# Hybrid decoder block, MLP stages: operands refilled two tiles to a slot, weight sums kept in DRAM, down's first units held in up's buffers

## The chip, the cores and the metric

The kernel runs on one core of one Trainium2 chip. The time is the device time of one execution in microseconds (us); the time of a kernel is the median of its runs. Everything is computed in float32.

## The reference

One layer of a decoder trunk over S = 2048 tokens of width D = 1024. The first half (projection, dilated attention, pooling groups) is not touched. What the change touches is the MLP behind it, with D_FF = 2816:

```python
h = h + concatenate([att, pool]) @ w_out
hn = _rmsnorm(h, ln_ffn)
up = _causal_dwconv(hn @ w_up, conv_w, conv_b)     # width 3, along the tokens, 2 * D_FF channels
gate, val = split(up, 2)
h = h + (silu(gate) * val) @ w_down
g = sigmoid(_rmsnorm(h, ln_ple) @ w_ple_gate)
h = h + g * (p @ w_ple)
return _rmsnorm(h, ln_final)
```

## The kernel before, in words

**Exact products.** Every float32 operand is split into a high part (a cast to fp32r by ScalarE, L83) and a low part (operand minus high part, a subtraction by VectorE or GpSimd, L84). A product is then three matmuls: high by high, high by low, low by high (L88 to L90 in `mm3`, L1236 in `product`). So each tile that TensorE uses needs one cast and one subtraction first.

**Stages.** Projection and attention come first. `phase_rest` then holds out projection, up, down, gate and final norm, one after the other.

**Out projection.** Four chunks of 512 tokens (`c`), each in two groups of four output banks (`grp`), eight steps of the contraction in the order 4, 5, 6, 7, 0, 1, 2, 3. The weights lie in a ring of ten tiles with the tag `w` (five pairs of high and low part) and a few more. A group's end adds the residual on VectorE, stores the new h (`h1`) through ScalarE's queue (L1118) and squares it on ScalarE (L153) for the norm; four steps later one-column matmuls (`st`, L99) sum the squares.

**Up's operands.** Up is computed by a Strassen-like scheme: the tokens fall into two halves of 1024, each half and the 1024 features of hn into 2 by 2 blocks, and seven products of block sums take the place of eight. `prepare(half)` normalises h1 and forms the seven operands a11, a12, a22, s1, s2, s3, s4, each of four tiles of 128 x 512. For half 0 it runs during the last chunks of the out projection: a11, s2, s1 and s4 are split at once and stay on the chip; a12, s3 and a22 go to DRAM (`g.op`). For half 1 all seven go to DRAM. `prepare` is a list of 22 small steps (`todo`), and two more are put in as it runs; in up, `product` pops one of them for each product from turn 1 on.

**Up.** 44 turns: two halves by 22 blocks of 128 gate channels and 128 value channels. A turn has seven slots, one product of 12 matmuls each, with these operands and weight blocks:

```text
slot 0  a11 x b11      slot 1  a22 x t4 (of the turn before)   slot 2  s2 x t2
slot 3  a12 x b21      slot 4  s1 x t1       slot 5  s3 x t3     slot 6  s4 x b22
```

Two weight tiles of 512 KB are loaded for a turn (`raw_load`, two turns ahead). GpSimd forms the sums t1, t3 (tile t13), t2 (in place in the first raw tile) and t4 (L1205 to L1207, L1214), again in half 1 as in half 0. The blocks are split in three pairs and one single (`split_w`). Slots 0, 2, 4 and 6 gather in one bank (`ua`), slot 3 in `ub`, slots 5 and 1 in `uc`. Along the way ScalarE copies the bank out before the next product is added (ug after slot 0, L1334, and after slot 2, L1352; uv after slot 4 and slot 6), so slot 2 cannot start before the ug copy; VectorE adds the other banks (L1261); the width-3 convolution is one scaled copy on ScalarE (`conv_a`, L1247) and four or two instructions on VectorE (`conv_b`, L1251 to L1258); silu, the product yg x yv (L1386), and the store to DRAM (`act`, L1387) follow in the next turn.

**What sets the order in up.** Up stands in a `manual_schedule` of TensorE, ScalarE, VectorE and GpSimd: these four run their instructions in the order in which the code writes them. Only SyncE, which issues most DMAs, is placed by the scheduler. `take_operand` fetches an operand's four tiles from DRAM through a ring of six tiles (`nt`) and splits them in one go, four casts one behind the other (L996) with their subtractions on VectorE and GpSimd in turn (L997). It does so for a12, s3 and a22 in turn 0, and for all seven operands of half 1 in turn 21 (the last, a22, in turn 22).

**Down.** Four chunks of 512 tokens by 22 units of the contraction. A unit is one weight tile (`ahead`, L1417) and one act tile (`act_ahead`, L1426), both loaded three units ahead and split; its seven products go to seven `dn` banks, the eighth to the bank `odd`, three units later (`wait = 3`), since the statistics matmuls of the chunk before (`fin`, two units into the next chunk) use that bank first. In chunk 2 `renorm` begins the norm for the gate; gate and final norm follow.

## Time and profile before

| | |
|---|---|
| runs | 2636.32, 2625.2, 2632.01 us; median 2632.01 |
| profiled execution | 2628.29 us, span in the trace 2626.5 us |
| mean granted clock of TensorE | 0.968 of full speed |
| TensorE busy | 2432.7 us (93% of the span) |
| VectorE, ScalarE, GpSimd busy | 1656.6, 1098.8, 705.3 us |
| out projection's last matmuls | until about 926 us of the span |
| up | about 926 to 1844 us |
| down, then gate and final norm | about 1861 us to the end |

How to read it: the execution's own time is 1.8 us longer than the span that the trace covers, and 3.7 us below the median of the runs. A matmul of 128 x 128 by 128 x 512 at the full clock comes every 0.2267 us. "Idle before" an instruction is the time in which its engine had nothing to do, with the engine or DMA that ended it behind the arrow. The granted clock of a stretch is a share of the full one.

### The profile page before, as it was taken

The page shows a single profiled execution, that of the slowest core. Times are in us where ns is not written, and L with a number is a line of the kernel's source. Part 1 is how long each engine was busy: PE and PEld are TensorE (multiplying, and loading weights), DVE is VectorE, ACT ScalarE, POOL GpSimd, SP SyncE. Part 2 cuts the span into 40 slices and gives each one's busy share as a digit, 9 for nine tenths or more (in the row PEclk, how much of TensorE's full clock was granted, in tenths as well). Part 3 has the DMA queues.
Part 4 walks back from the last instruction along what each step waited for, and adds up shares of the span by engine and source line. Part 5 has one row for each costly group of instructions (what it writes and reads, how often), then busy time and mean ns, then how long its engine had stood idle before and what let it go on. Part 6 is the DMA issues. An engine that isn't in the chain of part 4 may idle for free.

```text
span 2626.5 us, 31943 instructions
## 1 busy us (share of the span) xinstructions
PE 2432.7 (93%) x11515; PEld 2030.2 (77%) x11515; DVE 1656.6 (63%) x2404; ACT 1098.8 (42%) x1923; POOL 705.3 (27%) x534
## 2 busy tenths in 40 slices
PE   8999998877889978999996999999799999998998
PEld 7888887766768867788885877778687878787788
DVE  6635437876852668888887777777334363434655
ACT  5423228876821243444454444444223242323332
POOL 3312220244500152334345333332121222122000
PEclk9999999988989989999997999999899999999999
DMA  7534369768466646322223222221445464535332
GB/s 235 175 125 170 132 206 241 171 178 200 139 227 200 232 136 204 125 96 72 96 89 120 76 93 73 73 96 65 153 145 197 146 213 145 186 129 171 120 107 85
DMA packets 203822, 383.73 MB, mean 146 GB/s; under 512 B 37792, under 2 KB 80416, under 8 KB 200592
## 3 DMA queue, kind: packets, MB, share of 16 engines
q1 hardware_dynamic: 168608, 328.56, 39.8%
q0 software_dynamic: 18912, 25.75, 3.0%
q10 hardware_dynamic: 16144, 27.38, 2.8%
q8 instruction: 91, 1.49, 0.2%
q14 instruction: 67, 0.55, 0.1%
HBM read 272.71 MB, written 108.82 MB: 145 GB/s over the span
## 4 chain that ended last, share of the span: by engine, by line
PE 54%; DVE 14%; issue 11%; ACT 8%; DMA 7%; POOL 2%; SPq 0%; ACTq 0%; POOLq 0%; DVEq 0%
PE ua L1236 9%; PE dn L89 5%; PE dn L88 5%; PE dn L90 5%; PE uc L1236 4%; PE z L90 3%; PE z L88 3%; PE z L89 3%; ACT wu L83 3%; PE ub L1236 2%; DMA wb<-wd 2%; PE o L90 2%; DVE yg L1251 2%; DVE yg L1252 2%; PE o L88 2%
## 5 line engine op out<-in xcount | busy, mean ns | idle before, releaser
L88 PE MATMUL dn<-ah,hd 128*128 128x512 f32 x704 | 277.5, 394 | 16.9 <-ACT ah L83 16.9
L89 PE MATMUL dn<-al,hd 128*128 128x512 f32 x704 | 276.8, 393 | 0.9 <-DVE al L84 0.9
L90 PE MATMUL dn<-ah,ld 128*128 128x512 f32 x704 | 276.5, 393 | 0.0
L84 POOL TENSOR_TENSOR ld<-rd,hd 128x1024 fp32r<-128x1024 f32 x44 | 105.9, 2407 | 437.8 <-ACT hd L83 425.4
L83 ACT CAST hd<-rd 128x1024 fp32r<-128x1024 f32 x88 | 92.6, 1052 | 311.6 <-PE dn L89 171.3
L84 DVE TENSOR_TENSOR al<-ra,ah 128x512 fp32r<-128x512 f32 x88 | 124.5, 1418 | 137.4 <-ACT ah L83 137.4
L88 PE MATMUL z<-hnh,wh 128*128 128x512 f32 (+1 forms) x480 | 171.2, 357 | 9.6 <-ACT hnh L251 6.1
L89 PE MATMUL z<-hnl,wh 128*128 128x512 f32 (+1 forms) x480 | 170.8, 356 | 2.5 <-DVE hnl L252 2.3
L90 PE MATMUL z<-hnh,wl 128*128 128x512 f32 (+1 forms) x480 | 170.6, 355 | 1.7 <-POOL wl L84 1.7
L88 PEld LDWEIGHTS dn<-ah,hd 128*128 128x128 f32 x704 | 134.0, 190 | 45.3 <-ACT ah L83 17.3
L89 PEld LDWEIGHTS dn<-al,hd 128*128 128x128 f32 x704 | 133.9, 190 | 30.0 <-DVE al L84 2.2
L90 PEld LDWEIGHTS dn<-ah,ld 128*128 128x128 f32 x704 | 133.7, 190 | 28.1
L1205 POOL TENSOR_TENSOR t<-ru 128x512 f32<-128x512 f32 x44 | 59.5, 1352 | 350.8 <-DVE wu L84 335.2
L1236 PE MATMUL ua<-s2h,wu 128*128 128x512 f32 x352 | 121.9, 408 | 34.3 <-ACT ug L1334 34.3
L84 DVE TENSOR_TENSOR wu<-ru,wu 128x1024 fp32r<-128x1024 f32 x88 | 119.8, 1362 | 52.8 <-ACT wu L83 52.8
L84 DVE TENSOR_TENSOR wu<-t,wu 128x1024 fp32r<-128x1024 f32 x88 | 87.2, 991 | 100.8 <-ACT wu L83 58.6
L84 DVE TENSOR_TENSOR ld<-rd,hd 128x1024 fp32r<-128x1024 f32 x44 | 53.9, 1224 | 126.2 <-ACT hd L83 125.3
L154 DVE TENSOR_TENSOR acc<-acc,sq 128x512 f32<-128x512 f32 (+1 forms) x125 | 89.8, 719 | 58.3 <-ACT sq L153 46.0
L1236 PE MATMUL uc<-a22h,wu 128*128 128x512 f32 x352 | 118.1, 397 | 8.7 <-DVE uv L1261 8.6
L1236 PE MATMUL ua<-a11h,wu 128*128 128x512 f32 x352 | 117.6, 395 | 9.0 <-ACT wu L83 8.8
L1236 PE MATMUL ua<-s4h,wu 128*128 128x512 f32 x352 | 117.4, 395 | 4.8 <-ACT uv L1375 4.8
L1236 PE MATMUL ub<-a12h,wu 128*128 128x512 f32 x352 | 115.8, 390 | 0.0
(304 smaller groups left out, 6817.7 us busy)
## 6 DMA issues: line engine op xcount, KB each, us to landing
ru<-in_w_up_dram SPq DMA_DIRECT2D x88, 512.0 KB, 3.7
rd<-in_w_down_dram SPq DMA_DIRECT2D x88, 512.0 KB, 3.6
act<-yg SPq DMA_DIRECT2D x44, 512.0 KB, 2.9
ra<-act SPq DMA_DIRECT2D x88, 256.0 KB, 3.7
wr<-in_w_in_dram SPq DMA_DIRECT2D x64, 256.0 KB, 4.0
nt<-h SPq DMA_DIRECT2D x56, 256.0 KB, 3.6
h<-h SPq DMA_DIRECT2D x56, 256.0 KB, 5.2
qhh<-qh SPq DMA_DIRECT2D x16, 512.0 KB, 9.4
```

Of the source, the lines that this page charges most:

```text
L83: nc.scalar.copy(hi, src)
L84: (low or nc.gpsimd).tensor_tensor(lo, src, fp(hi), op=ALU.subtract)
L88: nc.tensor.matmul(ps, wh, ah, start=first, stop=False)
L89: nc.tensor.matmul(ps, wh, al, start=False, stop=False)
L90: nc.tensor.matmul(ps, wl, ah, start=False, stop=last)
L154: nc.vector.tensor_tensor(acc[:, :n], acc[:, :n], sq[:, :n], op=ALU.add)
L1205: eng.tensor_tensor(t13[:, :CH], r0[:, CH:], r0[:, :CH], op=ALU.subtract)
L1236: nc.tensor.matmul(pst, x[:, ksl], y, start=first and k == 0 and n == 0, stop=k == HK - 1 and n == 2, skip_group_check=True)
L1251: nc.vector.scalar_tensor_tensor(y[:, 1:], u[:, : n - 1], coef(f, 1), y[:, 1:], op0=ALU.mult, op1=ALU.add)
L1252: nc.vector.scalar_tensor_tensor(y[:, 2:], u[:, : n - 2], coef(f, 0), y[:, 2:], op0=ALU.mult, op1=ALU.add)
```

## The change

It has six parts. All six are in one kernel.

1. **Turn 0's weights earlier.** `raw_load(0)`, the sums and the splits of turn 0 stand inside the last chunk of the out projection: the sums behind the first group, the four splits behind the first four steps of the second group.
2. **Weight sums kept.** In half 0 each turn stores its t13, t2 and t4 to a new DRAM buffer, `g.td` (1 MB a turn: `keep_t`, `keep_t4`). In half 1 they are loaded from there; GpSimd forms none.
3. **Operands two tiles a slot.** `Refill` takes the place of `take_operand`: after a slot's copies it casts two operand tiles that were fetched six (half 0) or ten (half 1) tiles ahead, into the `nt` ring and, in half 1, the `inv` and `dg` buffers as well. Each third (half 0) or second (half 1) subtraction is GpSimd's, the others VectorE's. It runs over slots 0 to 5 of turn 0, slots 1 to 6 of turn 21 and all of turns 22 and 23 until its list is empty.
4. **Splits and steps spread.** The weight splits of the next turn stand at slots 2, 4 and 6 (in turn 0 at 4, 5 and 6) instead of 0, 3 and 6. The steps that prepare half 1 run after every fifth slot, from turn 2 on, instead of after every product from turn 1 on.
5. **Down's first units in up's buffers.** In the last turn (43), the weight and act tiles of down's units 0, 1 and 2 are loaded and split into the `w` ring and into tiles of the pools of a11 and s2. Those pools are closed only in unit 8 of down's first chunk.
6. **Down's buffers and waits.** Three more pairs of weight tiles (`wx`), eight instead of five act pairs, `wait = 5` instead of 3, the statistics matmuls five units into the next chunk instead of two, and the tick that counts them at a unit's head instead of behind it. The `dg` and `inv` tiles come from the stage's own pool.

The diff, cut to its core:

```diff
+            def raw_load(i):
...
+                if half == 0:
+                    nc.sync.dma_start(r0, w_up[f, 0])
+                else:
+                    nc.sync.dma_start(r0[:, :CH], w_up[f, 0][:, :CH])
+                    nc.sync.dma_start(r0[:, CH:], g.td[f][:, 1024 : 1024 + CH])
+                nc.sync.dma_start(r1, w_up[f, 1])
...
+                t13 = (pool or fb).tile([P, 1024], F32, tag="t13", name="t13")
+                if half:
+                    nc.sync.dma_start(t13, g.td[f][:, :1024])
+                    return
...
+        def keep_t(i):
+            if i < len(turns) and turns[i][0] == 0:
+                f = turns[i][1]
+                nc.sync.dma_start(g.td[f][:, :1024], ts[i][0])
+                nc.sync.dma_start(g.td[f][:, 1024 : 1024 + CH], raws[i][0][:, CH:])
...
+                if c == NCH - 1:
+                    raw_load(0)
+                    early = [("b11", "t2"), ("t1", "t3"), ("b22", "b21"), ("t4",)]
                 for grp in range(2):
                     begin(grp)
-                    part(grp, ks)
+                    if grp and early:
+                        for q, names in enumerate(early):
+                            part(grp, ks[q : q + 1])
+                            split_w(0, *names)
+                        part(grp, ks[len(early) :])
...
+                    if grp == 0 and early:
+                        sums_t(0, np0)
+                        sum_t4(0, cb)
...
-            if todo:
-                todo.pop(0)()
...
+            def take(self, n=1):
+                for _ in range(n):
...
+                    t = self.got.pop(0)
+                    nc.scalar.copy(hi, t)
+                    (nc.gpsimd if m % self.low == self.low - 1 else nc.vector).tensor_tensor(lo, t, fp(hi), op=ALU.subtract)
+                    if m:
+                        self.fetch()
...
+            refill = Refill(0, ("a12", "s3", "a22"), 6, 3)
...
+                if i == 2:
+                    prep.extend(prepare(1, fb, prep))
+                if i == NF - 1:
+                    refill = Refill(1, ("a11", "s2", "a12", "s1", "s3", "s4", "a22"), 10, 2)
+                    for _ in range(10):
+                        refill.fetch()
+                def after(slot):
+                    if i == 0 and slot < 6 or i == NF - 1 and slot > 0 or i in (NF, NF + 1):
+                        refill.take(2)
+                    if 2 <= i < NF - 1 and (7 * i + slot) % 5 == 0 and prep:
+                        prep.pop(0)()
+                def splits(slot):
+                    if i == 0:
+                        at = {4: (("b11", "t2"),), 5: (("t1", "t3"),), 6: (("b22", "b21"), ("t4",))}
+                    else:
+                        at = {2: (("b11", "t2"),), 4: (("t1", "t3"),), 6: (("b22", "b21"), ("t4",))}
...
+                if last:
+                    unit0 = first_units(0)
...
+        wait = 5
+        NX = 3
...
+                if kind == "d" and m % (NW + NX) >= NW:
...
+                    hi = fd.tile([P, 1024], F32R, tag="wx", bufs=2 * NX, name=f"hd{c}_{i}")
...
-                ah = fd.tile([P, CH], F32R, tag="ah", bufs=5, name="ah")
+                ah = fd.tile([P, CH], F32R, tag="ah", bufs=wait + 3, name="ah")
...
-            wait = 3
             for f in range(NF + wait):
                 n = c * NF + f
+                tk.tick()
...
-                tk.tick()
...
-            tk.later(2 if c < NCH - 1 else 6, fin)
+            tk.later(5 if c < NCH - 1 else 6, fin)
```

Three places show how the instructions move. Each row is a line of the kernel (before or changed, by its own numbers), the operation and its operands.

The first is ScalarE's program at the end of the out projection and in turn 0. `wu` are weight parts of up, `ru` and `t` what they are cast from, `sq` the squares of the out projection, `a12h` an operand's high parts. Before:

```order
L153 ACTIVATE sq<-xc_8919 128x512
L83 CAST wu<-ru 128x1024
L83 CAST wu<-t_9074 128x1024
L83 CAST wu<-ru_9067 128x1024
L83 CAST wu<-t_9078 128x512
L83 CAST wu<-ru 128x1024
L996 CAST a12h_9134<-nt 128x512
L996 CAST a12h_9136<-nt 128x512
L996 CAST a12h_9138<-nt 128x512
L996 CAST a12h_9140<-nt 128x512
L1334 COPY ug<-ua 128x512
```

With the change, in two pieces of the same program:

```order
L83 CAST wu<-ru 128x1024
L153 ACTIVATE sq<-xc_8767 128x512
L83 CAST wu<-t_8937 128x1024
L83 CAST wu<-ru 128x1024
L83 CAST wu<-t_8941 128x512
L1195 DMA h_231<-xc_8948 128x512
L153 ACTIVATE sq<-xc_8948 128x512
```

```order
L153 ACTIVATE sq<-xc_8952 128x512
L153 ACTIVATE sq<-xc_8954 128x512
L1338 CAST a12h_9155<-nt 128x512
L1338 CAST a12h_9159<-nt 128x512
L1419 COPY ug<-ua 128x512
L1338 CAST a12h_9169<-nt 128x512
L1338 CAST a12h_9175<-nt 128x512
```

Turn 0's four weight casts now stand ahead of the last group's squares, the fifth (turn 1's) is gone from this place, and two operand casts instead of four stand ahead of the ug copy.

The second is VectorE's program in a turn of half 1, from the add behind slot 1 on. `yg` and `yv` are the convolved gate and value, `ug` and `uv` what they are made from, `wu` a weight's low part. Before:

```order
L1261 TENSOR_TENSOR ug<-ug,uc 128x512
L84 TENSOR_TENSOR wu<-t_14131,wu 128x1024
L1261 TENSOR_TENSOR ug<-ug,ub 128x512
L1251 SCALAR_TENSOR_TENSOR yg<-ug,vec,yg 128x1023
L1252 SCALAR_TENSOR_TENSOR yg<-ug,vec,yg 128x1022
L1257 SCALAR_TENSOR_TENSOR yg<-halo,vec,yg 128x1
L1258 SCALAR_TENSOR_TENSOR yg<-halo,vec,yg 128x2
L1261 TENSOR_TENSOR uv<-uv,uc 128x512
L1386 TENSOR_TENSOR yg<-yg,yv 128x1024
L84 TENSOR_TENSOR wu<-ru_14024,wu 128x1024
L84 TENSOR_TENSOR wu<-t_14157,wu 128x512
L84 TENSOR_TENSOR wu<-ru,wu 128x1024
```

With the change:

```order
L1305 TENSOR_TENSOR ug<-ug,uc 128x512
L84 TENSOR_TENSOR wu<-ru,wu 128x1024
L1305 TENSOR_TENSOR ug<-ug,ub 128x512
L1295 SCALAR_TENSOR_TENSOR yg<-ug,vec,yg 128x1023
L1296 SCALAR_TENSOR_TENSOR yg<-ug,vec,yg 128x1022
L1301 SCALAR_TENSOR_TENSOR yg<-halo,vec,yg 128x1
L1302 SCALAR_TENSOR_TENSOR yg<-halo,vec,yg 128x2
L84 TENSOR_TENSOR wu<-t_14206,wu 128x1024
L1305 TENSOR_TENSOR uv<-uv,uc 128x512
L1472 TENSOR_TENSOR yg<-yg,yv 128x1024
L84 TENSOR_TENSOR wu<-ru_14098,wu 128x1024
L84 TENSOR_TENSOR wu<-t_14230,wu 128x512
```

The subtraction of the t1/t3 pair moved from ahead of the convolution of yg to behind it, and that of the b11/t2 pair from the turn's end to the place where t1/t3 stood, two slots later.

The third is SyncE's queue between up and down. `act` is the store of a finished block, `ra` the load of an act tile for down, `rd` that of a weight tile. Before:

```order
L933 DMA rd_4_15490<-in_w_down_dram 128x1024
L1387 DMA act_203<-yg 128x1024
L933 DMA rd_5_15525<-in_w_down_dram 128x1024
L933 DMA rd_6_15564<-in_w_down_dram 128x1024
L1387 DMA act_204<-yg 128x1024
L1430 DMA ra<-act_183 128x512
L1430 DMA ra<-act_184 128x512
L1430 DMA ra<-act_185 128x512
```

With the change:

```order
L1473 DMA act_224<-yg 128x1024
L1352 DMA ra<-act_205 128x512
L1352 DMA ra<-act_207 128x512
L1352 DMA ra<-act_206 128x512
L1349 DMA rd<-in_w_down_dram 128x1024
L933 DMA rd_3_15519<-in_w_down_dram 128x1024
L1473 DMA act_225<-yg 128x1024
L933 DMA rd_4_15552<-in_w_down_dram 128x1024
L1506 DMA rd<-in_w_down_dram 128x1024 x2
L1473 DMA act_226<-yg 128x1024
L1521 DMA ra<-act_208 128x512
L1521 DMA ra<-act_209 128x512
```

The act tiles of units 0 to 2 (L1352) are now loaded two stores ahead of up's last store; from the fourth unit on (L1521) they still stand behind it.

More of the change, by code (lines that the diff above doesn't have):

```diff
@@ L1324, in phase_rest @@
                     conv_a(prev.yv, prev.uv, NF + prev.f)
-                if not over:
-                    split_w(i + 1, "b11", "t2")
-                if i == 0:
-                    take_operand("a12")
+                after(0)
+                keep_t(i + 1)
                 if prev:
@@ L1367, in phase_rest @@
                     conv_b(prev.yg, prev.ug, prev.f, prev.half)
-                if i == NF - 1:
-                    take_operand("a12")
+                splits(4)
+                after(4)
+                if last:
+                    unit1()
+                    unit2 = first_units(2)
                 if not over:
```

266 lines of the change are left out of this document (148 added, 118 removed).

## The prediction

> **What bounds the kernel now.** I read the page first, then the table of stretches over the up, down and gate stages, then who waited for whom, then the timelines at the places where TensorE stood still.
>
> ```profile
> PE 2432.7 (93%) x11515; PEld 2030.2 (77%) x11515; DVE 1656.6 (63%) x2404; ACT 1098.8 (42%) x1923; POOL 705.3 (27%) x534
> ```
>
> TensorE is busy for 93% of the span, so a change can only win what TensorE loses. Ten stretches show where that is in the part that is edited (length, then busy time and count of each engine, granted clock, DMA share, GB/s):
>
> ```profile
> core 0: us, PE busy (x) PEld busy (x) DVE busy (x) ACT busy (x) POOL busy (x), PEclk, DMA share, GB/s
> 925.80:960.39 34.59, 20.13 (x70) 15.34 (x70) 22.10 (x20) 16.98 (x27) 22.04 (x16) 0.75 0.70 228
> 979.43:1092.95 113.52, 101.60 (x426) 81.12 (x425) 99.99 (x111) 47.00 (x58) 34.62 (x20) 0.97 0.53 176
> 1092.95:1359.51 266.56, 266.56 (x1178) 220.72 (x1177) 217.72 (x197) 124.92 (x154) 98.47 (x58) 1.00 0.25 83
> 1359.51:1426.28 66.77, 43.60 (x170) 34.96 (x169) 48.91 (x43) 33.18 (x50) 38.20 (x23) 0.80 0.42 134
> 1426.28:1819.70 393.42, 386.27 (x1682) 313.92 (x1681) 310.31 (x322) 180.39 (x220) 134.89 (x78) 1.00 0.23 79
> 1843.80:1866.00 22.20, 5.30 (x14) 3.63 (x13) 12.17 (x15) 6.43 (x8) 2.46 (x1) 0.62 0.56 187
> 1992.00:2012.00 20.00, 13.71 (x52) 11.14 (x51) 5.97 (x11) 4.54 (x7) 3.32 (x2) 0.74 0.68 241
> 2112.00:2122.00 10.00, 6.41 (x22) 4.83 (x21) 8.88 (x13) 6.44 (x10) 1.87 (x1) 0.83 0.92 298
> 2249.00:2269.00 20.00, 14.07 (x57) 11.52 (x56) 5.63 (x7) 4.54 (x7) 4.17 (x3) 0.83 0.59 212
> 2380.00:2403.00 23.00, 16.93 (x66) 12.30 (x65) 4.39 (x4) 9.90 (x12) 10.10 (x5) 0.96 0.87 289
> ```
>
> Row 3 is the measure: fourteen turns of 84 matmuls without a gap, 266.56 / 14 = 19.04 us a turn, 0.2267 us a matmul, 2.72 a slot. Against it the other rows lose: row 1 (end of the out projection to slot 6 of turn 0, five slots) 34.6 - 13.6 = 21.0; row 2 (five turns) 18.3; row 4 (two turns, the change of halves) 28.7; row 5 (twenty turns) 12.6; row 6 (up to down) 22.2 - 14 x 0.2267 = 19.0; rows 7 and 9 (ends of down's chunks) 8.2 and 7.1; row 8 5.0; row 10 (into the gate) 8.0. That is all there is to win: 128. From 1861 to 2372 the waits behind rows 6 to 9 have these names (sum, count, longest):
>
> ```profile
> PE dn L88 <- ACT ah L83: 16.9, 1, 16.9
> PE st L99 <- DVE acc L154: 12.2, 2, 6.3
> PE bc L136 <- DVE h L1458: 3.6, 1, 3.6
> ```
>
> **The change part by part.** *Entry of up.* Now slot 0 waits for the cast of turn 0's first weights, which load after the out projection, and slot 2 for a copy behind operand casts; the second row is ScalarE's wait before its last eviction, and the loads of those operands follow:
>
> ```profile
> 934.76 0.79 PE L1236 MATMUL ua<-a11h,wu 128*128 128x512 f32 x1 [8.83 <-ACT wu L83]
> ...
> 946.17 0.80 PE L1236 MATMUL ua<-s2h,wu 128*128 128x512 f32 x1 [5.50 <-ACT ug L1334]
> ```
> ```profile
> 925.71 0.63 ACT L153 ACTIVATE sq<-xc 128x512 f32<-128x512 f32 x1 [12.98 <-DVE xc L1117]
> ```
> ```profile
> L1270 SPq DMA_DIRECT2D nt<-op0a x4: 320/465/740, 926.9 to 930.0; - x4
> ```
>
> and from issue to landing
>
> ```profile
> DMA to landing us min/median/max: 2.9/6.4/7.5
> ```
> ```profile
> 930.00:940.00 10.00, 5.11 (x11) 3.61 (x12) 7.08 (x6) 4.09 (x5) 6.85 (x5) 0.51 0.89 315
> ```
>
> The four casts and subtractions of turn 0 move into the 13 us in which ScalarE idles before the last eviction, so they cost nothing (uncovered, about 4 us), and slot 0 follows the out projection at 925.8. The ug copy for slot 2 then has two a12 casts ahead of it, not four and more. Their loads go out at about 926.9 and take 6.4 less one 512 KB load that no longer stands before them (1.7 us at 315 GB/s): 931.6. With 0.5 for the second, 0.6 cast and 0.6 copy slot 2 starts at 933.3, 4.8 after slot 0 ends. A 6.3 us wait cost 8.2 in row 7, so I add 1.9 for the half clock, and 1.0 for the statistics matmuls: 7.7 is left of 21.0, **gain 13.3** (19 if the casts need not wait, 8 if they wait as long again).
>
> *Turns 2 to 6.* The 24 steps that prepare the second half come every fifth slot up to turn 20, not every slot.
>
> ```profile
> 1003.99 1.41 DVE L1034 SCALAR_TENSOR_TENSOR nt<-nt,vec,inv 128x512 f32<-128x512 f32 x2
> ```
> ```profile
> 1266.48 1.22 DVE L1386 TENSOR_TENSOR yg<-yg,yv 128x1024 f32<-128x1024 f32 x1
> ...
> 1268.75 0.68 DVE L84 TENSOR_TENSOR wu<-t,wu 128x512 fp32r<-128x512 f32 x1
> ```
> ```profile
> 1267.92 1.25 ACT L1247 ACTIVATE yv<-uv,vec 128x1024 f32<-128x1024 f32 x1
> 1269.07 1.03 ACT L83 CAST wu<-ru 128x1024 fp32r<-128x1024 f32 x1
> ```
> ```profile
> 1272.47 2.72 PE ua L1236 x12
> ```
>
> A step is about 1.4 us of VectorE, and a turn leaves it 19.04 - 217.72 / 14 = 3.5. The chain that matters runs from the product yg x yv through conv yv and the ug copy to slot 2 at 1272.47: with 0.6 for the copy it ends at 1270.7 now, 1.8 early. The b11 cast (1.03) leaves this chain and the t1 subtraction (1.2) goes behind the convolution on yg, so slack is near 4 us, more than one step takes. I leave 0.9 for the spread matmuls and 2 for collisions: **gain 15.4** of 18.3. Bounds: 17.4; or each step shows in full, 24 x 1.41 = 34, a loss of 16.
>
> *Change of halves.*
>
> ```profile
> 1402.30 0.62 ACT L996 CAST s4h<-nt 128x512 fp32r<-128x512 f32 x1 [3.51 <-DMA nt<-op1s]
> 1408.45 0.62 ACT L996 CAST s4h<-nt 128x512 fp32r<-128x512 f32 x1 [5.53 <-DMA nt<-op1s]
> ```
>
> ScalarE casts 28 operands in one go and waits for buffers; slot 1's eviction stands behind. Now ten buffers are filled ahead and two operands follow each slot's copies. Fourteen of the subtractions stay on VectorE: two turns of 15.6 plus 14 x 0.68 are 40.6 in 38.1 us, so 2.5 over, and s4's last pair is cast just before its slot: 4 is left of 28.7, **gain 24.7** (28.7 at best; 9 if the 20 us of waits on loads stay).
>
> *Second half.* POOL's four sums a turn become loads.
>
> ```profile
> 1652.61 1.28 DVE L1252 SCALAR_TENSOR_TENSOR yv<-uv,vec,yv 128x1022 f32<-128x1022 f32 x1
> 1653.81 0.21 DVE L1257 SCALAR_TENSOR_TENSOR yv<-halo,vec,yv 128x1 f32<-128x1 f32 x1
> ```
>
> ```profile
> 1660.84 2.19 DVE L1252 SCALAR_TENSOR_TENSOR yg<-ug,vec,yg 128x1022 f32<-128x1022 f32 x1
> 1662.95 1.24 DVE L1257 SCALAR_TENSOR_TENSOR yg<-halo,vec,yg 128x1 f32<-128x1 f32 x1
> ```
>
> The same two instructions take 1.49 without POOL and 3.43 beside it. Taking 1.9 off a chain that is 0.7 too long removes **all 12.6** (nothing, if something else holds ug). By the Trainium skill, SBUF — State Buffer, section Who interferes with whom, a VectorE instruction with two SBUF inputs contends with a GpSimd instruction that reads SBUF; the trace agrees with 2.19 against 1.28, and the rule speaks against the first half, where the sums now run beside other such instructions: that is the first rival. The stores (1 MB a turn, 55 GB/s) and loads (0.77 MB more a turn, 40 GB/s) lie beside DMA shares of 0.25 and 0.23; I cost them at nothing, and the third rival says what they cost uncovered.
>
> *Up to down.*
>
> ```profile
> 1855.90 0.33 SPq L1387 DMA_DIRECT2D act<-yg  x1
> 1856.28 2.21 SPq L1430 DMA_DIRECT2D ra<-act  x4
> ```
> ```profile
> 1860.41 1.26 ACT L83 CAST ah<-ra 128x512 fp32r<-128x512 f32 x2 [5.79 <-DMA ra<-act]
> ```
>
> Three units now lie in up's buffers: 3 x 21 x 0.2267 = 14.3 us of matmuls. The fourth still loads behind the last act store, so its cast ends as now at about 1861.0 (second of two, 0.62 each), 17.2 after up's end at 1843.8: 2.9 short, 1 more for the clock, **gain 15.1** of 19.0 (10 to 18). By the Trainium skill, TensorE: Matmul & The Clock Gate, Part 1, the clock falls after an idle window of about 3.4 us; by that the 1 goes. Row 10 has 0.96 with no single wait over 2 us, so the trace decides for a cost.
>
> *Down's chunks and the gate.*
>
> The statistics come three slots later, 3 x 4.76 = 14 us against waits of 6.3 and 5.9: rows 7 and 9 go, 15.3. The bc wait stays, less two tail slots (6 x 0.2267 = 1.4). **Gain 16.7** (12 to 20). Into the gate five weight units find free buffers earlier: 3 of 8.0 (0 to 6).
>
> Sum: 13.3 + 15.4 + 24.7 + 12.6 + 15.1 + 16.7 + 3 = 100.8. The profiled execution took 2628.3, 3.7 under the median of the three runs: 2628.3 - 100.8 = 2527.5 against it, 2531 as a median.
>
> **Rivals.** *First half bound by VectorE.* POOL's sums wait for the t1 split (their buffer), which now follows the convolution on yg, so they run beside the yg product, the other splits and conv yv.
>
> ```profile
> 1376.89 3.46 DVE L997 TENSOR_TENSOR s2l<-nt,s2h 128x512 fp32r<-128x512 f32 x2
> ```
>
> Such a subtraction took 1.73 here against 0.68 above. If that and the steps eat the slack, 20 turns lose 0.7 as the second half does now (14), and a quarter of the steps show (8): 2531 + 22 = 2553. Against it: those 4 us of slack.
>
> *The refill still waits.* SP issues in one order, and loads of td, stores of act and operand loads queue behind each other; if the casts still wait for loads, the change of halves keeps its 20 us and the entry its other 5: 2556. For it: 3.51 and 5.53; against it: ten buffers, two casts a slot.
>
> *Slower: the second half waits for its sums.* If each turn's load of t13, stuck behind the queue, lands too late for its split, and TensorE waits 5.53 a turn, 22 turns lose 122 and the 12.6 is not won: 2531 + 134 = 2665. It decides from 5.2 us a turn (the change then is 13 slower). Against it: the load is issued a turn, 19 us, ahead, and the longest landing above is 7.5.
>
> **How the numbers follow.** Forecast 0.73, first rival 0.14, second 0.08, slower 0.03, and 0.02 that several terms fail together and nothing measurable is left; 0.5% (13 us) is about what a measurement tells from no change. The bounds add to gains of 57 to 120 us, 2512 to 2575; I take the whole of it, which holds both middle cases. Faster 0.95, same 0.02, slower 0.03.
>
> **What would show it.** Right: turns of 19.04 in both halves, no POOL sums after turn 21, one wait of about 5 us before slot 2 of turn 0, at most 5 lost over turns 21 and 22, down starting at once and pausing about 3 at its fourth unit, no st waits in chunks 1 to 3. Wrong: first-half turns of 19.7 or more (first rival), ScalarE waits on nt at the change of halves (second), splits waiting for DMA from td (third).

## The result, and the profile after

The changed kernel takes 2540.76 us (median of four runs, 2534.66 to 2545.49) against 2629.89 us of the kernel before (median of four, 2625.2 to 2636.32): a ratio of 0.9658, 95% interval 0.9628 to 0.9688. The forecast was 2531 in a range of 2512 to 2575. The profiled execution took 2540.58 us, its span is 2538.8 us, 87.7 under that of before.

Section 1 of the page, to be held against the row of before:

```profile
PE 2415.9 (95%) x11515; PEld 2025.9 (80%) x11515; DVE 1595.0 (63%) x2408; ACT 1106.6 (44%) x1923; POOL 546.3 (22%) x442
```

The same 11515 matmuls, in a span that is 3.3% shorter. The stretches of the changed kernel, cut where the work changes: out projection; turn 0; turns 1 to 6; turns 7 to 20; turns 21 and 22; turns 23 to 42; the start of down; then, in down, the first chunk end, the place of the `bc` matmuls, and the second and third chunk end (same columns as in the prediction):

```profile
core 0: us, PE busy (x) PEld busy (x) DVE busy (x) ACT busy (x) POOL busy (x), PEclk, DMA share, GB/s
728.72:934.06 205.34, 195.76 (x813) 157.34 (x813) 99.75 (x140) 41.40 (x63) 20.95 (x16) 0.94 0.67 225
934.06:960.35 26.29, 20.42 (x82) 16.18 (x81) 18.26 (x18) 14.00 (x24) 11.52 (x8) 0.87 0.79 266
960.35:1082.24 121.89, 117.15 (x509) 96.45 (x508) 99.88 (x98) 57.97 (x71) 48.51 (x28) 0.99 0.40 142
1082.24:1348.80 266.56, 266.56 (x1177) 220.79 (x1176) 230.82 (x226) 128.58 (x154) 93.17 (x54) 1.00 0.54 186
1348.80:1393.08 44.28, 40.41 (x170) 32.44 (x168) 42.03 (x42) 31.59 (x48) 19.72 (x13) 0.96 0.66 218
1393.08:1773.89 380.81, 380.81 (x1681) 315.32 (x1680) 261.71 (x322) 183.72 (x222) 2.27 (x2) 1.00 0.37 121
1795.60:1821.00 25.40, 21.43 (x88) 17.25 (x88) 13.65 (x15) 8.22 (x11) 5.14 (x2) 0.93 0.59 193
1930.00:1950.00 20.00, 20.00 (x94) 16.67 (x93) 11.14 (x14) 7.22 (x11) 6.75 (x3) 1.00 0.83 280
2033.00:2053.00 20.00, 19.22 (x85) 15.61 (x84) 15.09 (x21) 9.56 (x15) 2.68 (x1) 1.00 0.82 269
2053.00:2073.00 20.00, 20.00 (x93) 16.67 (x93) 16.36 (x20) 10.27 (x16) 6.14 (x3) 1.00 0.87 290
2170.00:2190.00 20.00, 20.00 (x94) 16.67 (x93) 10.97 (x12) 8.33 (x12) 6.90 (x4) 1.00 0.78 264
```

Turns 23 to 42 are 380.81 / 20 = 19.04 us each, as turns 7 to 20 are. Down's three chunk ends (the rows from 1930, 2053 and 2170) are without a gap. The out projection of before, in the same cut, from its first matmul to its end:

```profile
729.10:925.80 196.70, 190.34 (x812) 153.11 (x812) 94.85 (x136) 37.76 (x59) 15.88 (x12) 0.97 0.63 209
```

From such rows and the first and last matmul of each stage, the two profiled executions differ like this (us; the two parts of down are parted by TensorE's lost time in its first 25 us):

| stretch | before | after | gain | forecast |
|---|---|---|---|---|
| up to the out projection | 729.1 | 728.7 | 0.4 | 0 |
| out projection | 196.7 | 205.3 | -8.6 | 0 |
| its end to turn 1 | 37.2 | 26.3 | 10.9 | 13.3 |
| turns 1 to 6 | 132.6 | 121.9 | 10.7 | 15.4 |
| turns 7 to 20 | 266.6 | 266.6 | 0 | 0 |
| turns 21 and 22 | 66.8 | 44.3 | 22.5 | 24.7 |
| turn 23 to the end of up | 415.3 | 402.7 | 12.6 | 12.6 |
| lost in the gap and in down's first 25 us | 19.2 | 5.6 | 13.6 | 15.1 |
| the rest of up's end to the gate's first product | 506.8 | 483.2 | 23.6 | 16.7 |
| gate to the end | 256.3 | 254.2 | 2.1 | 3 |
| sum | 2626.5 | 2538.8 | 87.7 | 100.8 |

(The rows are rounded.) This is one trace of each kernel. A second trace of the kernel before (experiment 11) has a span of 2616.2 us: its gate takes 250.6 us and its turns 21 and 22 take 64.7, so these two rows of the table are good to some 6 and 2 us only.

What TensorE still waited for in up, and then in down (engine, line, releaser: us in total, times, longest):

```profile
PE ua L1282 <- ACT ug L1419: 5.9, 1, 5.9
PE ua L1282 <- ACT uv L1461: 5.0, 2, 4.7
PE ua L1282 <- DVE s4l L1339: 3.5, 1, 3.5
```

```profile
PE dn L88 <- DVE ug L1305: 4.0, 1, 4.0
PE bc L136 <- DVE h L1548: 0.8, 1, 0.8
```

Four waits are left in up, in turns 0, 3 and 22. The first is the one that the prediction left (slot 2 of turn 0, behind the operand casts). ScalarE's timeline shows it:

```profile
941.65 0.62 ACT L1338 CAST a12h<-nt 128x512 fp32r<-128x512 f32 x1 [0.78 <-DMA nt<-op0a]
942.18 0.58 ACT L1419 COPY ug<-ua 128x512 f32<-128x512 f32 x1
```

The one in turn 3 was not forecast. VectorE's timeline there:

```profile
1012.47 0.69 DVE L122 TENSOR_TENSOR dg<-ident,ph 128x512 fp32r<-128x512 f32 x1 [10.78 <-PE bc L136]
1013.08 0.69 DVE L122 TENSOR_TENSOR dg<-ident,pl 128x512 fp32r<-128x512 f32 x1
```

VectorE stood 10.8 us ahead of a diagonal tile (`dg`), until a `bc` matmul of TensorE was done; the convolution and the adds of that turn queued behind. The wait in turn 22, on ScalarE:

```profile
1384.36 0.57 ACT L1461 COPY uv<-ua 128x512 f32<-128x512 f32 x1
1387.23 1.06 ACT L1463 ACTIVATE yg<-yg 128x1024 f32<-128x1024 f32 x1 [2.30 <-DVE halo L1299]
1388.19 1.12 ACT L1338 CAST s4h<-nt 128x512 fp32r<-128x512 f32 x2
```

The last pair of s4 is cast behind silu, which waits for the convolution. And the pause in down, on VectorE:

```profile
1796.10 1.28 DVE L1295 SCALAR_TENSOR_TENSOR yv<-uv,vec,yv 128x1023 f32<-128x1023 f32 x1 [0.54 <-ACT yv L1291]
1797.42 1.28 DVE L1296 SCALAR_TENSOR_TENSOR yv<-uv,vec,yv 128x1022 f32<-128x1022 f32 x1
1798.62 2.30 DVE L1301 SCALAR_TENSOR_TENSOR yv<-halo,vec,yv 128x1 f32<-128x1 f32 x1
1800.95 0.22 DVE L1302 SCALAR_TENSOR_TENSOR yv<-halo,vec,yv 128x2 f32<-128x2 f32 x1
1801.09 0.68 DVE L1305 TENSOR_TENSOR ug<-ug,uc 128x512 f32<-128x512 f32 x1
```

Down begins at once, and TensorE stops at its fourth output bank until VectorE has added up's last bank `uc`, behind four convolution instructions. That is not the wait for the fourth unit's load that was forecast.

### The profile page after: what moved, and what is told of

It reads as the page before. It is cut to its first block, busy times and chain, and to the rows that moved or that the text cites. A ratio compares the mean times of both kernels' runs of the same rounds, so it can differ in the third digit from the quotient of the medians.

```text
span 2538.8 us, 31947 instructions
## 1 busy us (share of the span) xinstructions
PE 2415.9 (95%) x11515; PEld 2025.9 (80%) x11515; DVE 1595.0 (63%) x2408; ACT 1106.6 (44%) x1923; POOL 546.3 (22%) x442
## 4 chain that ended last, share of the span: by engine, by line
PE 74%; issue 8%; DMA 6%; DVE 5%; ACT 3%; POOL 1%; SPq 0%; POOLq 0%; ACTq 0%; DVEq 0%
PE ua L1282 18%; PE uc L1282 9%; PE dn L88 6%; PE dn L90 6%; PE dn L89 6%; PE ub L1282 5%; PE z L90 4%; PE z L88 4%; PE z L89 4%; DMA wb<-wd 2%; PE gp L88 2%; PE gp L89 2%; PE gp L90 2%; PE o L88 2%; PE o L90 2%
## 5 line engine op out<-in xcount | busy, mean ns | idle before, releaser
L84 DVE TENSOR_TENSOR al<-ra,ah 128x512 fp32r<-128x512 f32 x88 | 117.2, 1335 | 136.7 <-ACT ah L83 136.7
L88 PEld LDWEIGHTS dn<-ah,hd 128*128 128x128 f32 x704 | 132.6, 188 | 31.6 <-DVE ug L1305 4.4
L89 PEld LDWEIGHTS dn<-al,hd 128*128 128x128 f32 x704 | 132.6, 188 | 27.5
L84 DVE TENSOR_TENSOR wu<-ru,wu 128x1024 fp32r<-128x1024 f32 x88 | 129.3, 1469 | 4.4 <-ACT wu L83 4.4
L1282 PE MATMUL uc<-s3h,wu 128*128 128x512 f32 x352 | 115.7, 390 | 0.0
L1282 PE MATMUL ua<-s1h,wu 128*128 128x512 f32 x352 | 115.5, 389 | 0.0
```

Of the source, the lines that this page charges most:

```text
L84: (low or nc.gpsimd).tensor_tensor(lo, src, fp(hi), op=ALU.subtract)
L88: nc.tensor.matmul(ps, wh, ah, start=first, stop=False)
L89: nc.tensor.matmul(ps, wh, al, start=False, stop=False)
L1282: nc.tensor.matmul(pst, x[:, ksl], y, start=first and k == 0 and n == 0, stop=k == HK - 1 and n == 2, skip_group_check=True)
```

## The experiments

Each is the changed kernel with one edit, unless it says otherwise. Lengths of stages are read as in the table above, from each experiment's own trace.

### 1. The spread ahead of the second diagonal

```diff
-                todo.insert(1, lambda: spread_one(c, dgs))
+                todo.insert(0 if half else 1, lambda: spread_one(c, dgs))
```

> In half 1's preparation the spread of the first norm scale is put ahead of the second scale's diagonal tiles, instead of behind them. Theory: turn 3 lost 7.1 us because VectorE, which had to write the second pair of diagonal tiles (L122), waited 10.8 us for a buffer that the first spread's matmuls held, and that spread stood one step, five slots, behind it. Then turns 3 and 4 fall to 19.04 and the time falls by 7.7 us against the changed kernel, to about 2533. Rival: turn 3 is where VectorE's work of the first half, with GpSimd's sums beside it, is too much. Then some turn of 2 to 6 still loses 5 us or more and the time stays at 2538 to 2541.

Measured: 2532.46 us (2529.03 to 2539.19), ratio 0.963 (0.9606 to 0.9653). Turns 1 to 6 of this kernel:

```profile
960.72:1076.03 115.31, 115.31 (x510) 95.35 (x508) 100.69 (x98) 57.78 (x71) 48.61 (x28) 1.00 0.42 150
```

Against 6 x 19.04 = 114.2 they lose 1.1 instead of 7.7, with the same work on VectorE; turn 3 loses nothing. So turn 3's loss was the buffer: two diagonal tiles, held until a step that the new pace put five slots later.

### 2. Turn 0's weights late again

```diff
-                if c == NCH - 1:
-                    raw_load(0)
+                if False:
...
-            raw_load(1)
+            for i in range(2):
+                raw_load(i)
+            sums_t(0)
+            sum_t4(0)
+            for names in (("b11", "t2"), ("t1", "t3"), ("b22", "b21"), ("t4",)):
+                split_w(0, *names)
```

> Turn 0's weights are loaded, summed, split and stored behind the out projection again, as before the change; all else as changed. Theory: these loads, stores and splits, put into the out projection, are what made it 8.7 us longer (205.5 us from its first to its last matmul against 196.8). Then it goes back to 196 to 199, the wait at the entry of up grows by about 10 to 12 (slot 0 waits for its cast, slot 2 for operands behind it), and the sum is within 4 us of the changed kernel: 2539 to 2545. Rival: the out projection's growth has another cause (the place of the diagonal and scale tiles, or the timing of transfers from run to run). Then it stays at 203 to 207, and the time is 2549 to 2553.

Measured: 2542.08 us (2540.97 to 2546.59), ratio 0.9666 (0.9646 to 0.9686). TensorE's waits from the out projection to turn 0:

```profile
PE ua L1279 <- ACT wu L83: 8.7, 1, 8.7
PE st L99 <- DVE acc L154: 5.9, 2, 4.0
```

The wait of slot 0 for its cast is back at 8.7. The out projection takes 202.7 us: it did not go back to 197, so the theory's account of it fell. What got longer there is mainly the first group of the last chunk: 23.8 and 24.3 us in the two traces of the kernel before, 25.2 to 29.1 in those with early weights, 28.5 in this one without them. So the early weights are not needed for the longer out projection, as far as one trace can tell. The time, though, lies in the theory's range and not in the rival's, because the entry lost less than either had it. From the out projection's last matmul to turn 1 this kernel takes 30.8 us, the changed one 26.1, the kernel before 37.0: the early weights are worth 4.7 of the entry's gain. The other 6.2 is what is left over; it is put down to the refill two tiles a slot, which no run takes alone.

### 3. GpSimd's sums in half 1 again

```diff
-                if half == 0:
+                if True:
                     nc.sync.dma_start(r0, w_up[f, 0])
...
-                if half:
-                    nc.sync.dma_start(t13, g.td[f][:, :1024])
-                    return
```

> Half 1 loads both raw weight tiles and has GpSimd form its four sums a turn again; the sums of half 0 are still stored. Theory of the prediction: GpSimd beside VectorE's convolution is what made turns 25 to 42 last 19.75 us. Then they last 19.6 to 19.8 again and the time rises by about 12 to 2553. Rival: what took the 0.7 us off was the new place of the weight splits (the b11 pair and the t1 pair later in the turn). Then all turns of the second half stay at 19.04 and the time stays at 2538 to 2543.

Measured: 2546.98 us (2544.27 to 2547.64), ratio 0.9683 (0.9661 to 0.9704). Turns 25 to 42:

```profile
1432.71:1775.43 342.72, 342.72 (x1513) 283.78 (x1512) 286.09 (x290) 164.57 (x198) 121.28 (x70) 1.00 0.24 82
```

342.72 / 18 = 19.04: not a gap, with GpSimd as busy as before the change and VectorE busier (286.1 us in these 18 turns; before the change 279.7, and 233.2 with it). The time lies between the two figures that were expected, because the loss is elsewhere: turns 21 to 23 lose 17.5 instead of 6.2. TensorE waits there six times for the low parts of refilled operands (9.8 us in all; once, 3.5, in the changed kernel). VectorE's groups show that the two engines still get in each other's way, at another place; these rows are this kernel's, in turns 25 to 42:

```profile
L1467 DVE TENSOR_TENSOR yg<-yg,yv 128x1024 f32<-128x1024 f32 x18 | 40.6, 2258 | 0.0
L1291 DVE SCALAR_TENSOR_TENSOR yv<-uv,vec,yv 128x1022 f32<-128x1022 f32 x17 | 37.3, 2196 | 0.6
L1291 DVE SCALAR_TENSOR_TENSOR yg<-ug,vec,yg 128x1022 f32<-128x1022 f32 x18 | 23.1, 1283 | 0.6
```

The slow ones are now the product yg x yv (2258 ns against 1219 in the changed kernel) and the convolution of yv (2196 against 1283); before the change it was the convolution of yg (2.19 in the prediction's rows). These are the places that the prediction's first rival named for the first half. The product stands on the chain that the prediction traced to slot 2 and grows by 1.0 us there, less than the slack of near 4 that the prediction worked out.

### 4. The weight splits at their old slots

```diff
-                        at = {2: (("b11", "t2"),), 4: (("t1", "t3"),), 6: (("b22", "b21"), ("t4",))}
+                        at = {0: (("b11", "t2"),), 3: (("t1", "t3"),), 6: (("b22", "b21"), ("t4",))}
```

> The weight splits of the next turn stand at slots 0, 3 and 6 again, as before the change (turn 0 as changed); the sums of half 1 are still loaded. Theory of the prediction: with GpSimd idle the second half needs no new order. Then turns 25 to 42 stay at 19.04, the time at 2538 to 2546, and only turns with operand refills or preparation steps may lose a few us. Rival: the place of the splits is what the second half needed. Then turns 25 to 42 last 19.3 to 19.8 and the time is 2546 to 2556.

Measured: 2560.76 us (2557.04 to 2562.24), ratio 0.9732 (0.9712 to 0.9752). Turns 7 to 20, and turns 25 to 42:

```profile
1084.29:1360.30 276.01, 270.13 (x1178) 219.79 (x1176) 234.99 (x229) 128.78 (x157) 92.63 (x53) 1.00 0.52 179
1449.30:1792.02 342.72, 342.72 (x1514) 283.78 (x1512) 231.66 (x289) 162.79 (x198) 0.00 (x0) 1.00 0.37 122
```

TensorE's waits in turns 7 to 20 are all of one kind, for the ug copy ahead of slot 2:

```profile
PE ua L1282 <- ACT ug L1420: 5.7, 6, 1.3
```

The second half needs no new order once GpSimd is idle: 19.04 a turn, as the prediction's theory had it. The time is 20 us worse for another reason: turns 7 to 20 lose 9.4 (changed kernel: 0), turns 1 to 6 lose 14.4 (7.7), turns 21 to 23 lose 12.8 (6.2).

### 5. The add ahead of the last convolution

```diff
+                if over:
+                    add(prev.ug[:, hi_], prev.c)
                 if prev:
                     conv_b(prev.yv, prev.uv, NF + prev.f, prev.half)
...
-                if prev:
+                if prev and not over:
                     add(prev.ug[:, hi_], prev.c)
```

> Behind up's last product, VectorE adds the bank of slot 1 to ug before it convolves yv, not behind it. Theory: down's pause of 4.0 us is a wait for that bank, which down's fourth output bank takes over and which VectorE frees only behind four convolution instructions; the wait for the fourth unit's load, which the prediction expected, lies hidden behind it. Then the pause in unit 0 goes, a wait of 1 to 4 us for the fourth unit's act tile appears instead, and the time falls by 2 to 5 us against the changed kernel. Rival: the bank was the only limit. Then no pause is left in down's first five units and the time falls by 6. Second rival: the add is not what frees the bank in time. Then the pause stays at 4.

Measured: 2533.11 us (2532.73 to 2535.99), ratio 0.9632 (0.9616 to 0.9648). TensorE's waits in down:

```profile
PE dn L88 <- ACT ah L83: 1.9, 1, 1.9
PE bc L136 <- DVE h L1550: 0.8, 1, 0.8
```

The pause at the bank is gone, and the wait for the fourth unit's act tile stands in its place, 1.9 us at 1807.3, where the prediction had 2.9. From up's end to the gate the kernel is 1.6 us shorter. Most of the other 5.7 us by which its span is under that of the changed kernel lies ahead of the edit: the out projection takes 200.3 us, 5.2 less. So the 7.6 by which the median is lower are not the edit's worth; the rows give it 1.6, under the 2 to 5 that were expected.

### 6. No first units

```diff
-                last = i == len(turns) - 1
+                last = False
```

> Down's first three units are loaded and split by down itself, as before the change; all else as changed. Theory of the prediction: the gap of 16.9 us between up and down comes back, with 2 us of slow clock, and the pause in unit 0 (6.3 us with its slow clock) goes under it: the time rises by 10 to 15, to 2551 to 2556. Rival: the gap was closed by something else in the change (more buffers, another order of the queue). Then it stays under 8 us and the time at 2541 to 2547.

Measured: 2551.19 us (2549.84 to 2559.17), ratio 0.9704 (0.9686 to 0.9722). In down:

```profile
PE dn L88 <- ACT ah L83: 17.1, 1, 17.1
```

The gap is back in full. Down's lost time behind it falls by 2.8, since the bank is free by then: the first units are worth 14.5 in the rows and 10 in the medians (this trace's out projection is 7.6 shorter than the changed kernel's).

### 7. Three units of delay again

```diff
-        wait = 5
+        wait = 3
...
-            tk.later(5 if c < NCH - 1 else 6, fin)
+            tk.later(2 if c < NCH - 1 else 6, fin)
```

(with the tick behind the unit again; the act pairs, tied to the delay, fall from eight to six)

> Down's eighth bank waits three units again and the statistics matmuls come two units into the next chunk, behind the unit, as before; the additional weight buffers and first units stay. Theory of the prediction: the two waits for the squares' sum (6.3 and 5.9 us) and their slow clock come back: the time rises by 15, to 2556, with waits of 5 to 7 us at two chunk ends. Rival: the waits were long because loads and casts in the chunk's first units were late, which the additional buffers and act pairs mend. Then the waits are under 2 us and the time stays at 2539 to 2546.

Measured: 2540.02 us (2537.8 to 2542.87), ratio 0.9656 (0.9641 to 0.967): no difference to the changed kernel, where 15 us were expected. The waits in down are there, half as long as before the change (6.5 against 12.2 us):

```profile
PE st L99 <- DVE acc L154: 6.5, 3, 3.0
PE dn L88 <- DVE ug L1305: 4.0, 1, 4.0
PE bc L136 <- DVE h L1548: 1.1, 1, 1.1
```

Down is 10.8 us longer than in the changed kernel, and the gate 7.7 shorter (246.5 against 254.2; the rest is the stages ahead). What the gate waits for, in the changed kernel and then in this one, from its first product on:

```profile
PE pl L90 <- POOL wpl L84: 1.7, 1, 1.7
PE pl L88 <- ACT wph L83: 1.6, 2, 1.0
PE gp L90 <- POOL lwg L84: 1.3, 1, 1.3
PE pl L90 <- DVE wpl L84: 0.5, 1, 0.5
```

```profile
PE pl L88 <- ACT wph L83: 0.8, 1, 0.8
PE pl L90 <- DVE wpl L84: 0.5, 1, 0.5
```

The gate's own weights are late in the changed kernel. SyncE's queue has the reason: their first load there stands 6.2 us behind the gate's first product (2284.58), in this kernel 4.7 ahead of it (2290.93):

```profile
2290.75 5.01 SPq L941 DMA_DIRECT2D rwg<-in_w_gate_dram  x2
```

```profile
2286.19 10.68 SPq L941 DMA_DIRECT2D rwg<-in_w_gate_dram  x2
```

So what the later statistics win at the chunk ends is for the most part given back in the gate. The gate's length does not rest on this pair alone: it is 253.3 to 256.3 us in the eight traces with five units of delay to the end, and 246.5 to 249.6 in the four with three units or with the catch-up of experiment 9. With three units it is also 4 to 10 us shorter than in the kernel before (250.6 and 256.3), so the change does win there as long as the delay does not spend it.

### 8. A preparation step in each slot

```diff
-                    if 2 <= i < NF - 1 and (7 * i + slot) % 5 == 0 and prep:
+                    if 2 <= i < NF - 1 and prep:
```

> The steps that prepare half 1 run after every slot from turn 2 on, not after every fifth. Theory of the prediction: VectorE can't take a step of 1.4 us in each slot, and turns 2 to 6 lose 14 to 18 us again, against 7.7 with the change: 2547 to 2552. Rival: the slack that the later splits give holds the steps, and the one large wait (VectorE for the diagonal's buffer) shrinks to a slot. Then turns 2 to 6 lose under 6 us and the time is 2534 to 2540.

Measured: 2543.82 us (2541.23 to 2546.05), ratio 0.9669 (0.9655 to 0.9684). Turns 1 to 6:

```profile
954.01:1082.77 128.76, 120.11 (x509) 97.23 (x508) 120.60 (x126) 57.39 (x71) 46.54 (x27) 0.97 0.68 228
```

128.76 - 114.24 = 14.5 lost, VectorE is busy for 94% of the stretch, and 7.6 of the 8.6 us that TensorE waits are for VectorE's adds; turn 3 has no wait. The pace is worth 6.8 against the changed kernel with its stall in turn 3, and 13.4 against the first experiment, which has none. The time is only 3 above, under the 2547 to 2552 that were expected; this trace's out projection took 200.6 us, 4.9 less than the changed kernel's.

### 9. The eighth bank catches up in the last chunk

```diff
-                    term(f - wait, KD - 1)
-                    units.pop(("d", c, f - wait)), acts.pop((c, f - wait))
+                    upto = f - wait + 1
+                    if c == NCH - 1 and f > 9:
+                        upto += min(wait - 1, (f - 8) // 2)
+                    while done < min(upto, NF):
+                        term(done, KD - 1)
+                        units.pop(("d", c, done)), acts.pop((c, done))
+                        done += 1
```

> In down's last chunk the eighth bank, which runs five units behind, catches up to one unit behind from unit 10 on (four units do two such products); all else as changed. Theory: what the later statistics won at the chunk ends (about 10.8 us in down's rows against a wait of three units) was given back in the gate (254.2 us against 246.5), because five units hold their weight tiles two units longer and the gate's weights load later. Then the gate's first loads into its own buffers come before its first matmul or shortly behind it, the gate takes 246 to 249 us, down stays where it was, and the time falls by 5 to 8 us. Rival: the gate is bound by the queue and its buffers, not by the tiles that are held. Then the gate stays at 253 to 255 and the time within 2 us.

Measured: 2532.75 us (2530.38 to 2533.49), ratio 0.9634 (0.9617 to 0.965). Down's lost time is unchanged (10.2 against 10.1), the gate takes 247.2, and its waits in the stretch that experiment 7 showed are down to the same two, 0.7 and 0.5. The gate's own weights now load 14.7 us ahead of its first product (2284.52):

```profile
2269.83 7.01 SPq L941 DMA_DIRECT2D rwg<-in_w_gate_dram  x2
```

This settles what the seventh left: tiles held by five delayed units kept the gate's weights from being loaded.

### 10. Four edits together

Experiments 1, 5 and 9, and a quicker refill in turn 21:

```diff
-                        refill.take(2)
+                        refill.take(3 if i == NF - 1 and slot > 3 else 2)
```

> Four edits to the changed kernel together: the spread ahead of the second diagonal, the add ahead of the last convolution, the eighth bank that catches up in the last chunk, and three instead of two operand tiles a slot in slots 4 to 6 of turn 21, so that s4 is split a slot before its product. Theory: each loss has a cause of its own, and the gains add: 7 (turn 3), 2 to 3 (down's start), 5 to 7 (gate) and 3 to 6 (turn 22): 2520 to 2524. Rival: the loads of turn 22 or the casts ahead of ScalarE's copies take the place of the s4 wait, and turns 21 and 22 still lose 5 or more: 2524 to 2530.

Measured: 2524.45 us (2520.42 to 2527.29), ratio 0.9602 (0.9584 to 0.9619). Two of the four edits gave what they gave alone (turns 1 to 6 lose 1.1, down 8.4). The catch-up gave less: the gate takes 249.6, where it took 247.2. The quicker refill gave little, as the rival had it: turns 21 and 22 lose 5.1 instead of 6.2, because another wait came up where s4's was:

```profile
PE ua L1282 <- ACT uv L1463: 2.4, 1, 2.4
```

### 11. The kernel before, once more

> The kernel before, unchanged, for a second trace of its out projection. Theory: the out projection's length varies from run to run with the timing of its transfers (197.6 to 205.5 us in nine traces whose out projection is the same program or differs only in turn 0's weights), and 196.8 in the one trace of before is one draw of it. Then this trace may show anything from 196 to 205. Rival: the change made it longer. Then it shows 196 to 197.5 again.

Measured: one run of 2618.08 us, out projection 196.6 us, while those of experiments 9 and 10, on the same chip, took 204.2 and 202.9. It goes with the rival: two traces of before agree, and every trace with the change is longer, by 1 to 9 us. Two draws do not rule out the theory.

### 12. The diagonal and scale tiles back in their old pool

The tenth kernel, with `dg` and `inv` in the pool of the whole phase again, as before the change (half 1's refills borrow them there):

```diff
-        aux[0] = cb
+        aux[0] = sb
...
-                inv[c] = pool.tile([P, CH], F32, tag="inv", bufs=2, name="inv")
+                inv[c] = (pool if c % 2 else sb).tile([P, CH], F32, tag="inv", bufs=1, name="inv")
```

> The four edits of the run before, and the diagonal and scale tiles lie in the pool of the whole phase again (as in the kernel before), which puts the out projection's other tiles back to the addresses they had; half 1's refills borrow these tiles there. Theory: the out projection got longer (196.6 and 196.8 us before, 197.6 to 205.5 in ten traces since, with early and with late weights of turn 0 alike) because its tiles moved, or because the scale and diagonal tiles' buffers set other waits. Then it takes 196 to 199 us and the time falls to 2518 to 2521. Rival: neither the place nor those tiles matter, and one late transfer early in the last chunks, which the queue's order hands on, draws the length anew in each run. Then it takes anything from 198 to 206, and the time stays at 2521 to 2527.

Measured: 2517.62 us (2517.18 to 2520.88), ratio 0.9572 (0.9558 to 0.9585), the fastest of all, 6.8 under the tenth; each of its five runs but one is under every run of that kernel. The out projection takes 199.4 us, on the edge between the two theories; the time, just under 2518, is nearer the first. Its first group is as short as before the change (36.4 us; 36.2 and 36.5 before, 36.9 to 38.4 in the traces between), but the first group of the last chunk is not (27.8; 23.8 and 24.3 before), and TensorE waits there as it did:

```profile
PE st L99 <- DVE acc L154: 4.5, 2, 3.2
```

The kernel before has 2.1 us in this row, the longest 1.2, and 3.2 with 1.8 in its second trace. The 3.2 here is the wait in the first group of the last chunk, where the kernel before waits 0.9 and 1.4; with the granted clock behind it (0.94 over the group, 1.00 before), that makes the 4 us by which the group is longer. Besides, down loses 1.4 us less and the gate takes 2.9 less than in the tenth, which the edit may or may not explain.

## Why the prediction was right, and where its steps were not

The likeliest case came in and the time lies in the range, 9.8 us above the point. Part of that closeness is luck: in the table six stretches gained 20.3 us less than forecast, and down's chunks won 6.9 more for a reason that the sum did not have. The stages, in order:

- **Entry: right, and its cover held.** Slot 0 follows the out projection at once, and one wait of 5.9 is left before slot 2. Over the six slots of turn 0 (16.3 us) 10.0 are left, where 7.7 were forecast: the wait is 1.1 longer than the 4.8 of the sum, and the slow clock behind it does most of the rest. That the early casts cost the out projection nothing fits experiment 2: without them it took 202.7, within the 197.6 to 205.5 of the traces that have them.
- **The out projection: not in the sum.** It got 8.6 longer in the profiled pair, which is two thirds of the 13.1 that are missing. The prediction took it as untouched. The early weights do not seem to be the cause (experiment 2); the moved tiles explain at most the first group (experiment 12); the longer wait for the squares' sum in the last chunk stays open.
- **Turns 2 to 6: the pace right, the collision missed.** "I leave 0.9 for the spread matmuls and 2 for collisions": the collision was one of 7.1, and not of VectorE's time but of a buffer. A step that frees the two diagonal tiles stood behind one that needs two more, and the new pace made of one slot five. Without it the loss is 1.1 (experiment 1), better than the 2.9 forecast; without the pace it is 14.5 (experiment 8).
- **Change of halves: right.** 6.2 is left, 4 was forecast, for the reason that it gave: s4's last pair is cast just before its slot. No cast waits for a load there any more, where the prediction's rows have waits of 3.51 and 5.53. But no run puts the old refill back, so that it won the 22.5 is read from the traces and not shown by undoing it; experiments 3 and 4 show that it needs the idle GpSimd and the new place of the splits as well.
- **Second half: the number right, the cause only half.** The sums' removal does make it 19.04 (experiment 4), but so does the new order alone (experiment 3). Two edits each removed the same 12.6. Experiment 3 gives what the removal is worth beside the order: 11.3 in turns 21 to 23, and nothing in the 18 turns for which it was counted. The first rival, a first half bound by VectorE, was a real danger: with the old splits it loses 16 more (experiment 4), and the waits of turns 7 to 20 are then those before slot 2, at the end of the chain whose slack the prediction held against this rival.
- **Up to down: the sum right, the wait another.** 13.6 against 15.1. The fourth unit's load was hidden behind a bank that VectorE freed late; with that mended, it shows as 1.9 (experiment 5). The prediction's 1861.0 is the end of the first of the two casts in its row, which is the right one; it calls it the second.
- **Down's chunks and the gate: a term too small in one place and spent in another.** In the rows down gained 23.6, not 16.7: the wait for the norm's spread, which was to stay, fell from 3.6 to 0.8. But the step from which the gain was worked out, statistics three units later, accounts for only 10.8 of it (experiment 7): with three units the waits are 6.5, not 12.2, so some 13 us come from something else in the change, which no run takes apart. And it is worth nothing in the time, since the gate gives back 7.7 (experiments 7 and 9). The forecast saw five weight units come free earlier there; it did not see that the delay holds two units more.

The third rival, loads of the sums that come late, has nothing for it: no split waits for a load in turns 23 to 42. Of the second rival, refills that wait, three casts in turn 0 show 3.3 us (two of a12 with 1.4, one of s3 with 1.9), and none in turns 21 to 23.

Two of the prediction's sums do not come out. The bounds that it gives term by term add to gains of 23 to 121.7 us, not 57 to 120, so they would have made the range 2510 to 2609. And the third rival decides from 4.6 us a turn, not 5.2, since the 12.6 that it also loses was left out there.

## What to carry to other kernels

When steps are spread further apart, look for buffers that are freed by one step and needed by the one before it: the hold grows with the pace. A delay that hides a wait at the head of a stage holds its tiles longer, so price it at the stage behind as well, and let it run out before the end. Where two edits serve the same wait, the trace of both says nothing on either: undo each alone.

## What the runs showed of the hardware

The out projection's length differed from trace to trace by up to 8 us among kernels with the same instruction order in it up to turn 0's weights (197.6 to 205.5), while two traces of the kernel before agree within 0.2 (196.6 and 196.8). Single times of these kernels can thus differ by more than some of the edits are worth, and the verdicts above rest on the rows of the stage that was edited.

Two VectorE instructions with two tensor inputs that run beside GpSimd's subtractions took 2196 ns on average instead of 1283, and 2258 instead of 1219, and TensorE lost nothing by it where there was slack for them (experiment 3).

The granted clock can fall after a wait of less than 2 us. In the fifth experiment, TensorE waited 1.9 us for the fourth unit and then worked without a gap; the row behind the wait:

```profile
1807.20:1812.00 4.80, 4.74 (x13) 3.51 (x14) 1.59 (x3) 1.25 (x3) 0.00 (x0) 0.64 0.86 278
```

Thirteen matmuls took the time of 21 at a granted clock of 0.64, so the wait of 1.9 us cost 3.8; the prediction was right to count a cost there (1 us; it was 1.9). By the Trainium skill, TensorE: Matmul & The Clock Gate, Part 1, the clock falls after an idle window of about 3.4 us. This row has it fall after a wait of 1.9.
